# Packing a mixture of experts: places counted in strips of 32, ranks of 96 beside ranks of 32

## The chip, the core and the metric

The kernel runs on one core of a Trainium2 chip. The engines that matter here are TensorE (PE, with its weight loads shown apart as PEld), VectorE (DVE), ScalarE (ACT), GpSimd (POOL) and SyncE (SP), whose queue issues the loads of weights. The metric is the device time of one execution in microseconds, the median of several runs.

## What is computed

Two layers follow each other on 512 tokens of 1024 features, all in float32. The first has a gated delta-rule mixer and then a mixture of experts; the second a state-space and convolution mixer and an MLP. The change touches the mixture of experts alone. In the reference it is:

```python
scores = sigmoid(hf @ router_w)                 # 64 experts
...                                             # groups, then the best 6 experts of a token
top_w = top_w / sum(top_w) * 2.5
def expert_block(args):
    tok, e = args
    return swiglu(h_pad[tok], w_gate[e], w_up[e], w_down[e])
...
routed = zeros((t + 1, d)).at[slot_tok].add(out * slot_w)[:t]
return routed + swiglu(hf, s_gate, s_up, s_down)   # the shared expert
```

An expert has gate and up matrices of 1024 x 256 and a down matrix of 256 x 1024, 3 MB together; 64 of them are 192 MB, and all are loaded once.

## The kernel before

**The plan.** How many tokens an expert gets is known only at run time. The kernel sorts the experts by that count, so rank 0 is the fullest, and gives each rank a fixed number of places (`CAPS`); tokens beyond them go to the loop `beyond`, which runs no turn on these inputs. Four experts (60 to 63) are `fix`ed: they have a block of 128 places of their own and come first, before the sorting is done. The other 60 ranks are laid into blocks of up to 128 rows by `plan()`: ranks 0 to 17 alone (`NPAIR`; ranks 0, 1 and 2 take two blocks each), ranks 18 to 43 in pairs, two strips of 64 rows to a block (`NQUAD`), and ranks 44 to 59 in fours, strips of 32. That makes 42 blocks: 4 fixed, 21 of one rank, 13 pairs, 4 fours. The list `BLOCKS` alternates blocks of one rank, fullest first, with blocks of several, emptiest first, so most of the stage is one-rank, pair, one-rank, pair; its last blocks are the pair of ranks 18 and 19 and then rank 17 alone.

**A block.** `blocks` (line 1638 and on) walks the list. For a block, `load_block` issues the loads of its experts' weights on SyncE's queue (line 1519; three loads of 1 MB an expert: two halves of gate and up, then down; first part 0 of every expert of the block, then part 1, then part 2). `gather` brings the tokens' rows (POOL, line 1587, two blocks ahead). `ffn` does the arithmetic: `pt_x` transposes the rows (line 142) and `modulate` writes `xT`; `gu` (line 139) has 8 steps over the features, in each of them one matmul for each strip of the block, 512 columns wide, gate and up side by side; ACT and DVE make `h`; `pt_h` transposes it; `py` has two halves of 512 columns, each with 2 steps and again one matmul a strip. A matmul of a strip of 32 or 64 rows has its place in the array by `tile_position=(0, a)`, where a is the strip's first row; a block of one rank has none. `scatter` (POOL, line 1633) adds each strip's rows to `yacc` in DRAM.

In the profile `gub<-ewrank,xTb 128*64` is such a matmul of `gu` with 64 rows, `pyb` one of `py`; `ewx` is a slot of the ring that was first another tensor. A float32 matmul has two records.

**What sets the order.** The code is written block by block; a scheduler then orders each engine's queue. In many pairs it issues `py` of the first strips, then the rest of the next block's `pt_x`, then the remaining `py`. The weights live in a ring of slots of 1 MB: 10, two more once the tables of places are made, three more from `SECOND` on (block 17 of the list, when two leave), and ten again in the last `LEAVE` = 6 blocks. A load waits until its slot's last reader is done and until the eighth load before it has landed.

The shared expert (`su`, `sg`, `spy`) is spread over the blocks by `hooks`. After the last block, `sums` are read back from `yacc`, added and normed, and PE goes on with `ptn` of the second layer.

The three lines of `ffn` around which the change turns are:

```python
m = n // len(ws)
parts = [(i * m, (i + 1) * m) for i in range(len(ws))]
...
    for (a, b), w in zip(parts, ws):
```

Of the kernel before, what the change touches and what calls it, by code (L numbers as in the profile page):

```python
# [16 lines left out]
P = 128  # L17
# [809 lines left out]
def block_one(k, pool, early, two, route):  # L827
# [7 lines left out]
    with ExitStack() as es:  # L835
# [217 lines left out]
NE = 64  # L1053
NFIX = 4
NRK = NE - NFIX
NPAIR, NQUAD = 18, 44
CAPS = [256, 192, 152, 128, 124, 118, 108, 100, 92, 88, 86, 82, 79, 76, 75, 72, 70, 68, 64, 64, 62, 62, 59, 57, 56, 54, 54, 52, 51,
        50, 49, 46, 45, 44, 44, 43, 42, 41, 41, 40, 39, 38, 37, 37, 32, 32, 32, 31, 30, 30, 28, 26, 25, 23, 22, 20, 20, 18, 17, 16]
CAPS = [-(-c // 16) * 16 for c in CAPS]
NOV = 72  # L1060
LEAVE = 6
LAST = 0
AHEAD = 2
RING = 10
RINGX = 3
# [4 lines left out]

def plan():

    fixed = [(e, P, [("fix", NRK + e)]) for e in range(NFIX)]
    one, more, b, r = [], [], NFIX, 0
    while r < NRK:
        n = 1 if r < NPAIR else 2 if r < NQUAD else 4
        c = CAPS[r]
        if n == 1:
            g = []
            while c > 0:  # L1080
                g.append((b, min(c, P), [("rank", r)]))
                c -= P
                b += 1
            one.append(g)
        else:
            more.append([(b, P, [("rank", r + i) for i in range(n)])])
            assert max(CAPS[r:r + n]) <= P // n
            b += 1
        r += n

    more = more[::-1]
    m = len(one) - LAST
    order, i, j = [], 0, 0
    while i < m or j < len(more):
        if i >= m or j < len(more) and j * m <= i * len(more):
            order.append(more[j])
# [12 lines left out]
CST2 = ["iota", "low", "col", "base", "cap"]


def const2():
    j = np.arange(P)[:, None]
    i = np.arange(P)[None, :]
    t = {
        "iota": np.broadcast_to(i, (P, P)),
        "low": (j < i),
        "col": np.broadcast_to(j, (P, P)),

        "base": np.broadcast_to(np.resize(np.concatenate([NFIX * P + np.cumsum([0] + STEP[:NRK - 1]), np.arange(NFIX) * P]), P)[:, None], (P, P)),  # L1120
        "cap": np.broadcast_to(np.resize(np.array(CAPS + [P] * NFIX), P)[:, None], (P, P)),
    }
    return np.concatenate([np.asarray(t[n], np.float32) for n in CST2], 1)
# [22 lines left out]
class Moe:  # L1146
# [423 lines left out]

    def parts(self, n):

        b, rows, whos = BLOCKS[n]
        if n < NFIX:
            return [(0, self.tokf[0:rows, b:b + 1])]
        if len(whos) == 1:
            return [(0, self.tok[0:rows, b:b + 1])]
        m = P // len(whos)
        t = {0: self.tok, 32: self.tok2, 64: self.tok3, 96: self.tok4}
        return [(a, t[a][0:CAPS[r], b:b + 1]) for a, (_, r) in zip(range(0, P, m), whos)]  # L1580

    def gather(self, idx):

# [5 lines left out]
                                            bounds_check=511, oob_is_err=False)  # L1589
        return X  # L1590

    def ffn(self, pool, ps, ws, X, wslot, n, nm):

        k, nc = self.k, self.k.nc
        xT = pool.tile([P, 8, P], F32, tag="xT", name="xT" + nm)
        for q in range(2):
            pt = ps.tile([P, 4, P], F32, tag="tp", name=f"pt_x{nm}{q}")
            for i in range(4):
                nc.tensor.transpose(pt[:, i, 0:n], X[0:n, (4 * q + i) * P:(4 * q + i + 1) * P], k.ident[0:n, 0:n])
            self.modulate(pt[:, :, 0:n], q, lambda c: xT[:, c, 0:n])  # L1600
        m = n // len(ws)
        parts = [(i * m, (i + 1) * m) for i in range(len(ws))]
        gu = ps.tile([P, 512], F32, tag="gu", name="gu" + nm)
        for i in range(8):
# [12 lines left out]
        y = pool.tile([P, 1024], F32, tag="y", name="y" + nm, bufs=3)  # L1617
        for half in range(2):
            cs = slice(512 * half, 512 * half + 512)
            py = ps.tile([P, 512], F32, tag="py", name=f"py{nm}{half}")  # L1620
            for c in range(2):
                for (a, b), w in zip(parts, ws):
                    nc.tensor.matmul(py[a:b, :], hT[:, c, a:b], w[2][:, c * 1024 + half * 512:c * 1024 + half * 512 + 512],
                                     start=(c == 0), stop=(c == 1), **({"tile_position": (0, a)} if len(ws) > 1 else {}))
            nc.vector.tensor_tensor(y[0:n, cs], py[0:n], self.gt2[0:n, cs], ALU.mult)  # L1625
        return y

# [9 lines left out]
    def blocks(self, bp, ps, hooks, span):  # L1637

        pend, Xs = self.pend, self.Xs
        for n in range(*span):  # L1640
            b, rows, whos = BLOCKS[n]
            if n == len(BLOCKS) - LEAVE:
                for f in self.first:
                    self.slots.remove(f)
            if n == len(BLOCKS) - LAST:

                last = [self.load(w[0]) for _, _, w in BLOCKS[n:]]
                for i in ((0, 1), (2,)):
                    for w in last:
                        for j in i:  # L1650
                            w[1](j)
            ws = self.load_block(whos)
# [12 lines left out]

    def beyond(self, bp, ps):
        k, nc, tc = self.k, self.k.nc, self.k.tc
        V = nc.vector
        n = nc.values_load(self.nov, min_val=0, max_val=NOV)
        with tc.For_i(0, n, 1) as i:  # L1670
            sl = bp.tile([P, 1], I32, tag="sl", name="sl_o")
            sw = bp.tile([P, 1], F32, tag="sw", name="sw_o")
            V.tensor_copy(sl, self.tok[:, bass.ds(i + NB, 1)])
            V.tensor_copy(sw, self.tw[:, bass.ds(i + NB, 1)])
            v = nc.sync.value_load(self.eov[:, bass.ds(i, 1)], min_val=0, max_val=NE - 1)
            src = k.I["ew"][bass.ds(v, 1)].rearrange("a p f -> p (a f)")
            ws = []
            for q in range(3):
# [739 lines left out]
def body(nc, tc, I, out, dbg=None):  # L2418
    k = Ctx()
    k.nc, k.tc, k.I, k.out = Nc(tc), tc, I, out  # L2420
    pool = lambda es, nm, bufs, **kw: es.enter_context(tc.tile_pool(name=nm, bufs=bufs, reuse_waits="tile", **kw))
    with ExitStack() as es:
# [11 lines left out]
        with ExitStack() as e1:  # L2434
# [7 lines left out]
            for _, _, whos in BLOCKS[:3]:  # L2442
                moe.load_block(whos)
# [32 lines left out]
```

## Time and profile before

| | us |
|---|---|
| median of three runs | 2032.55 |
| the runs | 2032.37, 2033.91, 2032.55 |
| the profiled execution | 2032.14 |
| its span in the trace | 2030.3 |
| PE busy | 1827.9 (90%) |
| ACT busy | 596.5 (29%) |
| DVE busy | 995.1 (49%) |
| POOL busy | 503.4 (25%) |

All durations below come from the one profiled execution, so sums are made against its 2032.14 us; 1.8 us of it lie outside the span. The page divides the span into 40 slices of 50.8 us and gives for each slice the busy share of every engine in tenths. A row of a timeline gives the start, the time from the first start to the last end of the instructions put together in it, the engine, the line, and what was written from what; its bracket says how long the engine was idle before and which engine it waited for. The mean granted clock of PE is 0.958 over the span.

### The profile page before, as it was taken

How to read it: one execution, taken by the hardware profiler on the slowest of the kernel's cores; microseconds unless marked ns; L12 is line 12 of the kernel's file. 1: busy time of each engine (PE TensorE's matmuls, PEld its weight loads, DVE VectorE, ACT ScalarE, POOL GpSimd, SP SyncE). 2: the span in 40 equal slices, each digit the busy share in tenths (PEclk: the TensorE clock that was granted, in tenths of full speed). 3: DMA queues.
4: the chain of work that ended last, by engine and by line, in shares of the span. 5: the costliest groups of instructions: out<-in, count | busy, mean ns of one | idle time of the engine just before them, and what ended most of it. 6: DMA issues, size and time to landing. Idle time of an engine off the chain costs nothing. (4 is left out here: it accounts for less than half of the span.)

```text
span 2030.3 us, 24186 instructions
## 1 busy us (share of the span) xinstructions
PE 1827.9 (90%) x8465; PEld 1235.3 (61%) x8465; DVE 995.1 (49%) x2205; ACT 596.5 (29%) x1124; POOL 503.4 (25%) x408
## 2 busy tenths in 40 slices
PE   5997778987889999989999984999999999999998
PEld 3785556876644333333333333888888788888886
DVE  4789955667866222352222226667433453323352
ACT  5443311213323111111111114343323334323441
POOL 1314343542322221212121215333100113101300
PEclk9998888997979999999999996999999999999999
DMA  8354353226478999999999973333332432333241
GB/s 309 122 184 148 89 161 97 81 71 215 157 295 297 354 370 351 346 392 389 365 369 370 374 267 114 122 94 92 108 99 84 134 100 94 93 94 104 78 140 42
DMA packets 135569, 394.01 MB, mean 194 GB/s; under 512 B 46932, under 2 KB 59348, under 8 KB 109080
## 3 DMA queue, kind: packets, MB, share of 16 engines
q1 hardware_dynamic: 109608, 363.60, 50.6%
q0 software_dynamic: 12016, 27.29, 5.5%
q10 hardware_dynamic: 13824, 1.58, 0.5%
q8 instruction: 67, 1.10, 0.2%
q14 instruction: 54, 0.44, 0.1%
HBM read 365.13 MB, written 39.06 MB: 199 GB/s over the span
## 5 line engine op out<-in xcount | busy, mean ns | idle before, releaser
L139 PE MATMUL gub<-ewrank,xTb 128*64 128x512 f32 (+5 forms) x960 | 266.4, 595 | 0.8 <-DMA ewrank<-ew 0.2
L274 DVE TENSOR_TENSOR wlo<-wraw,whi 128x1024 fp32r<-128x1024 f32 (+1 forms) x103 | 120.9, 1174 | 138.4 <-ACT whi L273 137.5
L139 PEld LDWEIGHTS gub<-ewrank,xTb 128*64 128x64 f32 (+5 forms) x960 | 89.0, 140 | 159.5 <-issue 146.7
L273 ACT CAST whi<-wraw 128x1024 fp32r<-128x1024 f32 (+1 forms) x115 | 113.9, 991 | 211.9 <-PE psi L139 50.6
L139 PE MATMUL pyb<-ewrank,hTb 128*64 128x512 f32 (+5 forms) x440 | 154.6, 609 | 3.3 <-DMA ewrank<-ew 1.3
L139 PE MATMUL psi<-xnh,whi 128*128 128x512 f32 (+1 forms) x368 | 142.6, 388 | 0.0
L139 PE MATMUL psi<-xnl,whi 128*128 128x512 f32 (+1 forms) x368 | 141.1, 384 | 0.0
L1633 POOL DMA_INDIRECT yacc<-yb,tok x63 | 89.0, 1412 | 171.3 <-DVE yb L1625 121.5
L1611 DVE SCALAR_TENSOR_TENSOR hb<-gub,tw,sgb 128x256 f32<-128x256 f32 (+5 forms) x38 | 18.3, 482 | 230.8 <-ACT sgb L1609 230.8
L1335 ACT ACTIVATE xTb<-pt_xb,B,A 128x128 f32<-128x128 f32 (+5 forms) x168 | 74.1, 445 | 170.3 <-DVE xTb L1337 169.0
L139 PE MATMUL psi<-xnh,wlo 128*128 128x512 f32 (+1 forms) x296 | 113.2, 383 | 0.0
L1587 POOL DMA_INDIRECT X<-hrow,tok x38 | 39.5, 1041 | 292.0 <-PE pt_xb L142 286.4
L1337 DVE TENSOR_SCALAR xTb<-pt_xb,A,B 128x128 f32<-128x128 f32 (+5 forms) x168 | 65.6, 393 | 89.3 <-PE pt_xb L142 52.9
L2399 POOL TENSOR_TENSOR fr<-fr 128x512 f32<-128x512 f32 x32 | 48.6, 1519 | 238.2 <-ACT fr L2398 238.2
L139 PE MATMUL psf<-xml,whi 128*128 128x512 f32 (+1 forms) x272 | 102.5, 377 | 0.2 <-DVE xml L274 0.2
L139 PE MATMUL psf<-xmh,whi 128*128 128x512 f32 (+1 forms) x272 | 102.4, 377 | 0.2 <-ACT xmh L273 0.2
L139 PE MATMUL psf<-xmh,wlo 128*128 128x512 f32 (+1 forms) x272 | 102.4, 377 | 0.0
L1609 ACT ACTIVATE sgb<-gub 128x256 f32<-128x256 f32 (+5 forms) x42 | 16.0, 382 | 262.4 <-PE gub L139 262.4
L139 PEld LDWEIGHTS pyb<-ewrank,hTb 128*64 128x64 f32 (+5 forms) x440 | 46.7, 143 | 76.0 <-issue 64.7
L1625 DVE TENSOR_TENSOR yb<-pyb,gt 128x512 f32<-128x512 f32 (+5 forms) x84 | 58.0, 690 | 70.2 <-PE pyb L139 70.0
L139 PEld LDWEIGHTS psi<-xnh,whi 128*128 128x128 f32 x368 | 69.9, 191 | 13.8 <-ACT xnh L2264 0.4
L139 PEld LDWEIGHTS psi<-xnl,whi 128*128 128x128 f32 x368 | 70.0, 190 | 13.2
(752 smaller groups left out, 4026.0 us busy)
## 6 DMA issues: line engine op xcount, KB each, us to landing
ewrank<-ew SPq DMA_DIRECT2D x168, 1024.0 KB, 25.1
wraw<-w_in SPq DMA_DIRECT2D x59, 512.0 KB, 3.6
wraw<-ff SPq DMA_DIRECT2D x32, 512.0 KB, 3.5
wf<-ff SPq DMA_DIRECT2D x64, 256.0 KB, 2.7
wm<-w_mod SPq DMA_DIRECT2D x28, 512.0 KB, 7.8
ewfix<-ew SPq DMA_DIRECT2D x12, 1024.0 KB, 15.4
ewx<-ew SPq DMA_DIRECT2D x12, 1024.0 KB, 20.2
wm<-w_mod SPq DMA_DIRECT2D x10, 1024.0 KB, 6.2
```

Of the source, the lines that this page charges most:

```text
L139: return self._done(self.eng.matmul(out, lhsT, rhs, **kw), rate, rhs)
L273: nc.scalar.copy(hi, raw)
L274: (eng or nc.vector).tensor_tensor(lo, raw, hi.bitcast(F32), ALU.subtract)
L1335: nc.scalar.activation(dst(c), pt[:, i, :], AF.Identity, scale=sa, bias=sb)
L1337: nc.vector.tensor_scalar(dst(c), pt[:, i, :], sa, sb, ALU.mult, ALU.add)
L1587: self.k.nc.gpsimd.indirect_dma_start(out=X[0:idx.shape[0]], out_offset=None, in_=self.hrow, in_offset=bass.IndirectOffsetOnAxis(ap=idx, a ...
L1609: nc.scalar.activation(sg[0:n], gu[0:n, 0:256], AF.Silu)
L1611: nc.vector.scalar_tensor_tensor(h[0:n], gu[0:n, 256:512], wslot[0:n], sg[0:n], ALU.mult, ALU.mult)
L1625: nc.vector.tensor_tensor(y[0:n, cs], py[0:n], self.gt2[0:n, cs], ALU.mult)
L1633: self.k.nc.gpsimd.indirect_dma_start(out=self.yacc[self.nsc % 2], out_offset=bass.IndirectOffsetOnAxis(ap=idx, axis=0), in_=y[a:a + n], i ...
L2399: nc.gpsimd.tensor_tensor(r, r, r, ALU.mult)
```

## The change

Places are counted in strips of 32: `STRIPS` gives each rank 8, 6, 5, five times 4, ten times 3, 26 times 2 and 16 times 1, and `CAPS` is 32 times that, nowhere less than before. `plan()` lays ranks into blocks without holes: rank 0 has two blocks; ranks 1 and 2 with one rank of 32 share three (128 of rank 1; 64 of rank 1 and 64 of rank 2; 96 of rank 2 and 32 of rank 44); ranks 3 to 7 have one each; ranks 8 to 17, of 96 places, share their block with one rank of 32 each; 26 ranks of 64 make 13 pairs; the five ranks of 32 that are left make one block of four and one block of rank 59 alone. That is 39 blocks: 4 fixed, 9 of one rank, 14 of two strips of 64, 1 of four, 11 of 96 and 32. A block's entry now holds the first row and the length of each part. In `ffn` a part of 96 rows becomes two strips, 64 and 32.

The list still alternates groups of `few` and `many`, but the groups are longer: after rank 59 alone and rank 0 come the four, two pairs, the three blocks of ranks 1, 2 and 44, four pairs, rank 3, three pairs, rank 4, four pairs, rank 5, and then the blocks of 96 and 32 with ranks 6 and 7 among them; the last is that of ranks 8 and 45.

```diff
-NPAIR, NQUAD = 18, 44
-CAPS = [256, 192, 152, 128, 124, 118, 108, 100, 92, 88, 86, 82, 79, 76, 75, 72, 70, 68, 64, 64, 62, 62, 59, 57, 56, 54, 54, 52, 51,
...
-CAPS = [-(-c // 16) * 16 for c in CAPS]
-NOV = 72
+
+STRIPS = [8, 6, 5] + [4] * 5 + [3] * 10 + [2] * 26 + [1] * 16
+CAPS = [32 * s for s in STRIPS]
+NOV = 73
...
+        for r in ranks:
+            base[r], n = P * b[0] + at, CAPS[r]
+            todo.remove(r)
+            while n > 0:
+                if at % P == 0:
+                    g.append((b[0] + at // P, []))
+                m = min(n, P - at % P)
+                g[-1][1].append((at % P, m, ("rank", r)))
+                at, n = at + m, n - m
...
+    few += [group([0]), group([1, 2] + ones(1))] + [group([r]) for r in range(3, n4)]
+    for n in (3, 2, 1):
+        while any(STRIPS[r] == n for r in todo):
+            g = [r for r in todo if STRIPS[r] == n][:{3: 1, 2: 2, 1: 4}[n]]
+            many.append(group(g + (ones(1) if n == 3 else [])))
...
-        m = n // len(ws)
-        parts = [(i * m, (i + 1) * m) for i in range(len(ws))]
+
+        strips = [(a + i, min(a + m, a + i + s), w) for (a, m, _), w in zip(parts, ws)
+                  for i, s in ([(0, 64), (64, 32)] if m == 96 else [(0, m)])]
...
-            for (a, b), w in zip(parts, ws):
+            for a, b, w in strips:
                 nc.tensor.matmul(gu[a:b, :], xT[:, i, a:b], w[i // 4][:, (i % 4) * 512:(i % 4) * 512 + 512],
-                                 start=(i == 0), stop=(i == 7), **({"tile_position": (0, a)} if len(ws) > 1 else {}))
+                                 start=(i == 0), stop=(i == 7), **({"tile_position": (0, a)} if len(strips) > 1 else {}))
```

The same is done in `py`. `parts`, `base` and the loop over blocks follow the new form of an entry; the branch for `LAST`, which was 0, goes.

Rank 8 shows what this does on PE. Before, in its own block 15, with 96 rows and no place in the array (`gub15`, `pt_hb15`, `pyb15`; the last number of a name is the program's own, and x4 are four in a row):

```order
L139 MATMUL gub15_7310<-ewrank8_0_7282,xTb15_7291 96x512 x4
L139 MATMUL gub15_7310<-ewrank8_1_7284,xTb15_7291 96x512 x4
L142 MATMUL pt_hb15_7323<-cst_60,hb15_7321 128x96 x2
L139 MATMUL pyb150_7329<-ewrank8_2_7286,hTb15_7326 96x512 x2
L139 MATMUL pyb151_7333<-ewrank8_2_7286,hTb15_7326 96x512 x2
```

After, in block 14 with rank 45, the first steps of `gub14`:

```order
L139 MATMUL gub14_8806<-ewrank8_0_8775,xTb14_8787 64x512
L139 MATMUL gub14_8806<-ewrank8_0_8775,xTb14_8787 32x512
L139 MATMUL gub14_8806<-ewrank45_0_8777,xTb14_8787 32x512
L139 MATMUL gub14_8806<-ewrank8_0_8775,xTb14_8787 64x512
L139 MATMUL gub14_8806<-ewrank8_0_8775,xTb14_8787 32x512
L139 MATMUL gub14_8806<-ewrank45_0_8777,xTb14_8787 32x512
```

Each step has now a matmul of 64 rows and one of 32 rows with rank 8's weights and one of 32 rows with rank 45's.

The second place is `py` of a block of two ranks that the scheduler divides. Before, the pair of ranks 18 and 19, on PE near the end of the stage:

```order
L139 MATMUL pyb250_8760<-ewrank18_2_8707,hTb25_8757 64x512
L139 MATMUL pyb251_8766<-ewrank18_2_8707,hTb25_8757 64x512
L142 MATMUL pt_xb241_8801<-cst_60,X2_4567 128x80 x2
L139 MATMUL pyb250_8760<-ewrank19_2_8709,hTb25_8757 64x512
L139 MATMUL pyb250_8760<-ewrank18_2_8707,hTb25_8757 64x512
L139 MATMUL pyb250_8760<-ewrank19_2_8709,hTb25_8757 64x512
L139 MATMUL pyb251_8766<-ewrank19_2_8709,hTb25_8757 64x512
L139 MATMUL pyb251_8766<-ewrank18_2_8707,hTb25_8757 64x512
L139 MATMUL pyb251_8766<-ewrank19_2_8709,hTb25_8757 64x512
```

After, PE's last block of the stage, ranks 8 and 45:

```order
L139 MATMUL pyb140_8841<-ewrank8_2_8783,hTb14_8838 64x512
L139 MATMUL pyb140_8841<-ewrank8_2_8783,hTb14_8838 32x512
L139 MATMUL pyb141_8849<-ewrank8_2_8783,hTb14_8838 64x512
L139 MATMUL pyb141_8849<-ewrank8_2_8783,hTb14_8838 32x512
L139 MATMUL pyb140_8841<-ewrank45_2_8785,hTb14_8838 32x512
L139 MATMUL pyb140_8841<-ewrank8_2_8783,hTb14_8838 64x512
L139 MATMUL pyb140_8841<-ewrank8_2_8783,hTb14_8838 32x512
L139 MATMUL pyb140_8841<-ewrank45_2_8785,hTb14_8838 32x512
L139 MATMUL pyb141_8849<-ewrank45_2_8785,hTb14_8838 32x512
L139 MATMUL pyb141_8849<-ewrank8_2_8783,hTb14_8838 64x512
L139 MATMUL pyb141_8849<-ewrank8_2_8783,hTb14_8838 32x512
L139 MATMUL pyb141_8849<-ewrank45_2_8785,hTb14_8838 32x512
```

Where strips of 64 alternated with strips of 64, the widths now go 64, 32, 64, 32 in the first four and change again in the other eight.

The third place is SyncE's queue where rank 0 comes. Before, from the loads of the four to rank 1's first parts:

```order
L1519 DMA ewx1_4984<-ew 128x2048
L1519 DMA ewrank57_2_5154<-ew 128x2048
L1519 DMA ewrank58_2_5156<-ew 128x2048
L1519 DMA ewrank59_2_5158<-ew 128x2048
L1519 DMA ewrank0_0_5258<-ew 128x2048
L1519 DMA ewrank0_1_5260<-ew 128x2048
L1519 DMA ewrank0_2_5262<-ew 128x2048
L1519 DMA ewrank1_0_5387<-ew 128x2048
```

After, from rank 59 alone to the middle of the four's first parts:

```order
L1522 DMA ewrank59_0_5108<-ew 128x2048
L1522 DMA ewrank59_1_5110<-ew 128x2048
L1522 DMA ewrank59_2_5112<-ew 128x2048
L1522 DMA ewrank0_0_5176<-ew 128x2048
L1522 DMA ewrank0_1_5178<-ew 128x2048
L1522 DMA ewrank0_2_5180<-ew 128x2048
L1522 DMA ewrank55_0_5326<-ew 128x2048
L1522 DMA ewx1_4984<-ew 128x2048
L1522 DMA ewx1_4984<-ew 128x2048
L1522 DMA ewrank58_0_5330<-ew 128x2048
L1522 DMA ewrank55_1_5332<-ew 128x2048
```

The four's loads stood ahead of rank 0's; now rank 0's stand ahead of them, and rank 59's ahead of those.

## Rows read from the trace of the kernel before

**Rows 1.** The page's second part: busy tenths of PE and DMA in 40 slices.

```profile
PE   5997778987889999989999984999999999999998
...
DMA  8354353226478999999999973333332432333241
```

**Rows 2.** The windows of the expert stage: busy us, granted clock, DMA share, GB/s.

```profile
680.00:720.00 40.00, 36.95 (x154) 14.26 (x153) 9.91 (x21) 7.22 (x18) 7.70 (x6) 1.00 0.94 321
...
760.00:800.00 40.00, 37.62 (x173) 15.47 (x173) 8.40 (x17) 6.53 (x15) 8.22 (x7) 1.00 0.86 340
...
840.00:880.00 40.00, 34.72 (x134) 13.81 (x132) 23.00 (x108) 6.47 (x15) 7.71 (x7) 1.00 0.90 326
880.00:1200.00 320.00, 291.05 (x1030) 106.84 (x1031) 83.68 (x188) 56.36 (x136) 67.64 (x53) 0.99 1.01 372
```

**Rows 3.** SyncE's timeline, 590 to 1190: start, us from first to last, count.

```profile
855.57 326.96 SPq L1519 DMA_DIRECT2D ewrank<-ew  x108
...
1100.45 82.09 SPq L1519 DMA_DIRECT2D ewrank<-ew  x27
```

**Rows 4.** The page's sixth part: loads of experts, KB each, us to landing.

```profile
ewrank<-ew SPq DMA_DIRECT2D x168, 1024.0 KB, 25.1
```

**Rows 5.** PE's timeline at the end of the expert stage: start, us, names.

```profile
1187.98 7.09 PE L139 MATMUL gub<-ewrank,xTb 128*64 128x512 f32 x32
...
1197.09 1.93 PE L139 MATMUL pyb<-ewrank,hTb 128*64 128x512 f32 x4
...
1199.23 3.65 PE L139 MATMUL pyb<-ewrank,hTb 128*64 128x512 f32 x12
1202.81 7.09 PE L139 MATMUL gub<-ewrank,xTb 128*80 128x512 f32 x16
...
1211.68 3.66 PE L139 MATMUL pyb<-ewrank,hTb 128*80 128x512 f32 x8 [0.44 <-ACT hTb L1616]
1248.20 2.39 PE L142 MATMUL ptn<-cst,sums 128*128 128x128 f32 x10 [32.85 <-ACT sums L2255]
```

**Rows 6.** The groups of instructions from 880 to 1200, weight loads of gub.

```profile
L139 PEld LDWEIGHTS gub<-ewrank,xTb 128*64 128x64 f32 (+3 forms) x528 | 52.4, 144 | 98.6 <-issue 90.5 <-DMA ewrank<-ew 4.5 <-ACT xTb L1335 3.4
```

**Rows 7.** PE's timeline earlier in the stage: one expert, four, a pair.

```profile
661.65 7.11 PE L139 MATMUL gub<-ewrank,xTb 128*128 128x512 f32 x16 [0.22 <-DMA ewrank<-ew]
...
674.68 1.88 PE L139 MATMUL gub<-ewrank,xTb 128*128 128x512 f32 x4
...
766.17 7.07 PE L139 MATMUL gub<-ewrank,xTb 128*32 128x512 f32 x64
...
840.09 7.09 PE L139 MATMUL gub<-ewrank,xTb 128*64 128x512 f32 x32
...
852.83 3.70 PE L139 MATMUL spy<-ewshared,shh 128*128 128x512 f32 x8
...
856.81 1.45 PE L139 MATMUL gub<-ewrank,xTb 128*128 128x512 f32 x3
```

**Rows 8.** PE's timeline where widths change, weight load (PEld) of pw last.

```profile
816.21 1.90 PE L139 MATMUL pyb<-ewrank,hTb 128*32 128x512 f32 x4
818.04 1.98 PE L139 MATMUL spy<-ewshared,shh 128*128 128x512 f32 x4
819.96 0.62 PE L139 MATMUL pyb<-ewrank,hTb 128*32 128x512 f32 x1
...
1295.79 1.92 PE L139 MATMUL pf<-smQ,smbst 128*16 128x128 f32 x16
...
1296.23 1.47 PE L139 MATMUL pf<-smQ,smbst 128*16 128x128 f32 x12
1297.64 1.20 PE L139 MATMUL pw<-ssU,smwin 128*64 128x64 f32 x32
...
1297.64 0.26 PEld L139 LDWEIGHTS pw<-ssU,smwin 128*64 128x64 f32 x6 [0.21 <-issue]
```

**Rows 9.** POOL's timeline at the end of the stage, the last scatter.

```profile
1216.35 1.42 POOL L1633 DMA_INDIRECT yacc<-yb,tok  x1 [9.33 <-DVEq L1670]
```

More of the change, by code (lines that the diff above doesn't have):

```diff
@@ L1055 @@
 NRK = NE - NFIX
-NPAIR, NQUAD = 18, 44
-CAPS = [256, 192, 152, 128, 124, 118, 108, 100, 92, 88, 86, 82, 79, 76, 75, 72, 70, 68, 64, 64, 62, 62, 59, 57, 56, 54, 54, 52, 51,
-        50, 49, 46, 45, 44, 44, 43, 42, 41, 41, 40, 39, 38, 37, 37, 32, 32, 32, 31, 30, 30, 28, 26, 25, 23, 22, 20, 20, 18, 17, 16]
-CAPS = [-(-c // 16) * 16 for c in CAPS]
-NOV = 72
+STRIPS = [8, 6, 5] + [4] * 5 + [3] * 10 + [2] * 26 + [1] * 16
+CAPS = [32 * s for s in STRIPS]
+NOV = 73
 LEAVE = 6
-LAST = 0
 AHEAD = 2
@@ L1071, in plan @@
 def plan():
[L1073 to L1096, printed above, removed]
+    few, many, base, todo = [], [], {}, list(range(NRK))
+    b = [NFIX]
+    def group(ranks):
+        g, at = [], 0
+        for r in ranks:
[7 more added lines that the diff above has]
+                at, n = at + m, n - m
+        b[0] += len(g)
+        return [(i, max(a + n for a, n, _ in ps), ps) for i, ps in g]
@@ new lines, in plan @@
+    n4 = sum(s > 3 for s in STRIPS)
+    ones = lambda n: [r for r in todo if STRIPS[r] == 1][:n]
+    few += [group([0]), group([1, 2] + ones(1))] + [group([r]) for r in range(3, n4)]
[3 more added lines that the diff above has]
+            many.append(group(g + (ones(1) if n == 3 else [])))
+    many = many[::-1]
+    order, i, j = [(e, P, [(0, P, ("fix", NRK + e))]) for e in range(NFIX)], 0, 0
@@ L1097, in plan @@
+    while i < len(few) or j < len(many):
+        if i >= len(few) or j < len(many) and j * len(few) <= i * len(many):
+            order += many[j]
             j += 1
         else:
-            order.append(one[i])
+            order += few[i]
             i += 1
-    order += one[m:]
-    return fixed + [x for g in order for x in g], b
-BLOCKS, NB = plan()
+    return order, b[0], [base[r] for r in range(NRK)]
+BLOCKS, NB, BASE = plan()
 NBT = NB + NOV
 NSLOT = NB * P
-STEP = [-(-c // P) * P if r < NPAIR else 64 if r < NQUAD else 32 for r, c in enumerate(CAPS)] + [P] * NFIX
@@ L1118, in const2 @@
         "col": np.broadcast_to(j, (P, P)),
-        "base": np.broadcast_to(np.resize(np.concatenate([NFIX * P + np.cumsum([0] + STEP[:NRK - 1]), np.arange(NFIX) * P]), P)[:, None], (P, P)),
+        "base": np.broadcast_to(np.resize(np.array(BASE + [P * e for e in range(NFIX)]), P)[:, None], (P, P)),
         "cap": np.broadcast_to(np.resize(np.array(CAPS + [P] * NFIX), P)[:, None], (P, P)),
@@ L1571, in parts @@
     def parts(self, n):
-        b, rows, whos = BLOCKS[n]
+        b, rows, ps = BLOCKS[n]
         if n < NFIX:
             return [(0, self.tokf[0:rows, b:b + 1])]
-        if len(whos) == 1:
-            return [(0, self.tok[0:rows, b:b + 1])]
-        m = P // len(whos)
         t = {0: self.tok, 32: self.tok2, 64: self.tok3, 96: self.tok4}
-        return [(a, t[a][0:CAPS[r], b:b + 1]) for a, (_, r) in zip(range(0, P, m), whos)]
+        return [(a, t[a][0:m, b:b + 1]) for a, m, _ in ps]
     def gather(self, idx):
@@ L1590, in gather, with ffn @@
         return X
-    def ffn(self, pool, ps, ws, X, wslot, n, nm):
+    def ffn(self, pool, ps, ws, X, wslot, n, parts, nm):
         k, nc = self.k, self.k.nc
@@ L1621, in ffn @@
             for c in range(2):
-                for (a, b), w in zip(parts, ws):
+                for a, b, w in strips:
                     nc.tensor.matmul(py[a:b, :], hT[:, c, a:b], w[2][:, c * 1024 + half * 512:c * 1024 + half * 512 + 512],
-                                     start=(c == 0), stop=(c == 1), **({"tile_position": (0, a)} if len(ws) > 1 else {}))
+                                     start=(c == 0), stop=(c == 1), **({"tile_position": (0, a)} if len(strips) > 1 else {}))
             nc.vector.tensor_tensor(y[0:n, cs], py[0:n], self.gt2[0:n, cs], ALU.mult)
@@ L1640, in blocks @@
         for n in range(*span):
-            b, rows, whos = BLOCKS[n]
+            b, rows, parts = BLOCKS[n]
             if n == len(BLOCKS) - LEAVE:
@@ L1644, in blocks @@
                     self.slots.remove(f)
[L1645 to L1652, printed above, removed]
+            ws = self.load_block([w for _, _, w in parts])
             self.rows_ahead(min(n + AHEAD, NFIX if span[0] == 0 else len(BLOCKS)))
-            y = self.ffn(bp, ps, ws, Xs[n], (self.twf if n < NFIX else self.tw)[:, b:b + 1], rows, f"b{b}")
+            y = self.ffn(bp, ps, ws, Xs[n], (self.twf if n < NFIX else self.tw)[:, b:b + 1], rows, parts, f"b{b}")
             part = self.parts(n)
@@ L1682, in beyond @@
             X = self.gather(sl)
-            y = self.ffn(bp, ps, [ws], X, sw, P, "o")
+            y = self.ffn(bp, ps, [ws], X, sw, P, [(0, P, None)], "o")
             self.scatter(y, [(0, sl)])
@@ L2441, in body @@
             ps = Psum(pool(e1, "psM", 1, space=PSUM), tp=3, gu=2, py=3)
-            for _, _, whos in BLOCKS[:3]:
-                moe.load_block(whos)
+            for _, _, parts in BLOCKS[:3]:
+                moe.load_block([w for _, _, w in parts])
             moe.places(ps, bp.tile([P, 1024], F32, tag="y", name="keys", bufs=3))
```

## The prediction

> **What bounds the kernel now.** I read the slices of the whole span first, 50.8 us each [rows 1]: TensorE (PE) stands at eights and nines from the 13th slice (609 us) on, but for the 25th (1218 to 1269), and the DMA tenths are nines from the 14th to the 23rd, some 510 us. That stretch is the expert stage, the only one the change touches. The windows of it [rows 2] say that it is close to a tie: from 880 to 1200 PE is busy 291 of 320 us and the DMA share is 1.01; in three earlier windows the share falls to 0.94, 0.86 and 0.90, so transfers also lose time. Then SyncE's queue: the last 27 loads of 1 MB are issued in 82.09 us, 82.09/26 = 3.16 us from one to the next, and 108 in 326.96 us, 3.06 [rows 3]; I take 3.14 for a load near the end. The last issue is at 1182.5, a load lands 25.1 us after its issue, so near 1207, and PE ends the last block at 1215.3 [rows 3 to 5]. On the other side the weight loads of `gub` wait only 4.5 us for transfers in those 320 us [rows 6]. So PE's own work decides, with transfers a few us behind it; whichever of the two grows sets the end. What follows (scatter, sums, `ptn` 32.85 us after PE's last) hangs on the last `pyb` [rows 5].
>
> **The change, part by part.** All is set against the profiled execution, 2032.14 us (span 2030.3), 0.4 us under the median 2032.55.
>
> *Blocks removed.* A block costs PE much the same whatever its strips, since strips of one width run side by side: `gub` takes 7.11 us for one expert, 7.07 for four strips (64 records), 7.09 for two (32) [rows 5, 7]. From one `gub` to the next: 13.03 for one expert (661.65 to 674.68); 14.83 for a pair whose `pyb` is issued in two pieces, 1.93 + 3.65 (1187.98 to 1202.81); 13.1 for a pair issued in one (840.09 to 856.81 is 16.72, less 3.6 of the shared expert's `spy` in it) [rows 5, 7]. A block of four goes as 13.1: same `gub`, same kind of `pyb`.
> Before: 21 x 13.0 + 4 x 13.1 + 2 x 13.1 + 11 x 14.83 = 514.7 us. After, were 96+32 like a pair: 9 x 13.0 + 1 x 13.1 + 7 x 13.1 + 7 x 14.83 (14 blocks of two strips of 64) + 10 x 14.83 + 1 x 13.1 = 487.0. That is **-27.7 us** of PE. Which are issued in one piece I counted in the order of the instructions.
>
> *The 96+32 blocks.* Eleven of them issue strips of 64, 32 and 32 in turn, 24 matmuls in `gub`, two records each. No block before mixes widths on disjoint columns, so the price must be bounded. Lower end: the strips overlap as equal ones do, and this costs nothing (below nothing is excluded, since no strip takes fewer records than the 0.43 us steps already counted). Upper end: PE waits for each width to finish. Three rows speak to it. Between 32-wide `pyb` and 128-wide `spy`, 816.21 to 818.04 is 1.83 and 818.04 to 819.96 is 1.92 us [rows 8]; four records there span 1.90 with 0.6 of the last, so a step is 0.43, eight are 3.43 and each change of width costs (3.75 - 3.43)/2 = 0.16. From 16-wide `pf` to 64-wide `pw`, four `pf` records take 0.44 (1295.79 to 1296.23), 0.11 each; twelve more should end at 1297.55 and `pw` starts at 1297.64, 0.09 later; its weight load starts only at 1297.64 too, put down to "issue", where other weight loads run ahead [rows 8]. So a change of width holds even the weight load until the array is empty. These rows have shared columns, so they show the wait and not that disjoint columns wait also. But a wait that keeps back the weight load looks like one of the whole array, and I take the upper end as likeliest, with 0.13 per change (mean of 0.09 and 0.16).
> The Trainium skill ("TensorEngine Tiling (Array Packing)", Tiling Modes, Key Properties) says that changing the tiling mode, not just the tile, drains TensorE. It speaks against this change; the rows on the changes of width agree as far as they go, and by it the sum is the upper end, without it the lower.
> Price: in `gub`, each of 8 steps has the 64 alone and then the two 32s together: 8 x (4 records x 0.429 + 2 x 0.13) = 15.8 against 7.09, +8.7. In `pyb` the first piece (64, 32, 64, 32) has four turns of 0.858 (two records) and four changes, 3.95 against 1.93, +2.0; the second has six turns and five changes, 5.8 against 3.65, +2.15. So +12.9 a block, 27.7 instead of 14.83, and **+142 us** for eleven. With 25 changes a block, 0.09 instead of 0.13 gives -11, 0.16 gives +8.
>
> *Transfers.* The same 192 MB of experts are loaded, in another order. A 96+32 block needs two experts, 6 x 3.14 = 18.8 us, under its 27.7: there the ring stays full and PE waits for nothing. In the first 23 blocks of ranks, up to the run of mixed ones, 111 loads x 3.14 = 349 us stand against PE's 328 of expert blocks (the sum above up to there) and some 58 of the shared expert's (four of 16 matmuls like a `gub`, eight like `spy`, 3.7 [rows 7]); level on the whole, but pairs now come four in a row (75 us of loads against 52 to 59 of PE). PE waits between nothing (10 to 13 slots loaded ahead cover a run) and 23 us (one run, nothing ahead); I take **+8**, nearer to the 4.5 of now [rows 6].
>
> *Tail and small edits.* The last block scatters two parts instead of one; POOL's last one takes 1.42 us [rows 9]: **+1.4**. SyncE reads experts' numbers ahead of loads as before. Gathers fall from 42 to 39 and scatter parts stay 67, on a POOL idle most of the stage; the tables are 2 columns smaller; new capacities are no smaller, so the overflow loop still runs no turn. Nothing for these: PE's block time hides them, and they only shrink.
>
> *Sum:* -27.7 + 142 + 8 + 1.4 = +123.7, and 2032.14 + 123.7 is about **2156 us**.
>
> **Rivals.**
> *A: the strips overlap, or a change costs its 0.13 alone.* Then a 96+32 block takes PE 14.8 to 18.1 (25 x 0.13), under the 18.8 of its loads, and transfers set the end: the 27.7 us buy nothing, as the same megabytes follow one another. What they lose decides. Rank 0's three slots are held through two blocks, 26 us, while only nine of the next four-block's twelve loads fit in the ring beside it: I reckon 15 us of idle queue near 666 to 680, some of it already lost now in the 0.86 and 0.90 windows [rows 2], and 4 to 8 more where two single experts no longer alternate with pairs. By slots and 3.14 a load the last landing comes some 16 us later; PE then needs 5 us after it instead of 8 to 9, since only the last `pyb` is left: +12, and +1.4. That is **2045**, slower too, but by 0.6%. For it: equal strips do overlap [rows 5, 7]. Against: the weight load that did not run ahead [rows 8].
> The Trainium skill ("TensorE: Matmul & The Clock Gate", Part 3) has column tiles run concurrently, with 3 tiles of 32 some 2.4 times faster. This trace agrees for equal widths, where the 16 + 16 records of a pair fit in 7.09 us; for 64 beside 32 no run here shows it. Were it so, rival A's time follows.
> *B: overlap, and the queue loses nothing: faster.* The place is the ring's refill at rank 0 and in the two low windows: 760 to 800 loses 0.14 x 40 = 5.6 us, 840 to 880 4.0, 680 to 720 2.4 [rows 2], together 12.0. If fewer one-expert blocks let the ring run at 1.01 throughout, the last landing comes 12 earlier and PE follows in 5 us instead of 8 to 9, -15.5, with the +1.4 to **2018**. It decides where a 96+32 block stays under 18.8 us and rank 0's hold costs under some 10 us.
>
> **How the numbers follow.** The forecast, drain: 0.70, with 2138 to 2179 as its own range (-11 and -8 for cheap changes and no waits, +8 and +15 the other way). A: 0.20. B: 0.05. Something between A and B, within 4 us (0.2%, about what a measurement of this kernel can tell from no change): 0.05. So faster 0.05, same 0.05, slower 0.90. For 8 in 10 the forecast's range alone is short, so it reaches down past A with some 7 us for its transfer terms, to 2038; what is left out is B, the middle and the edges.
>
> **What would show it.** In the changed kernel, `gub` of a 96+32 block near 15.8 us and block to block near 27.7; the 64 strip's record starting only after the 32s of the step before. If those `gub` take 7.1, A or B holds: then look at DMA's share from 640 to 760 and at the last landing against PE's end. One-expert blocks and pairs must stay at 13.0 and 13.1 to 14.8, and the tail from the last `pyb` to `ptn` at 32.9 + 1.4. Wrong would be the forecast also if PE's clock fell in the mixed blocks, or if loads, now ahead, still made PE wait.

## The result

The changed kernel takes 2172.34 us (2169.29 to 2174.51), the kernel before 2032.46 beside it: a ratio of 1.0695, 95% interval 1.068 to 1.0709. The forecast was 2156 in a range of 2038 to 2179, slower. Its profiled execution has a span of 2171.6 us, 141.3 more than before.

The slices of the changed kernel, 54.3 us each, against [rows 1] (first PE's busy tenths, then DMA's):

```profile
PE   6988599878799899888999998399999999999998
...
DMA  7454362254677959899976662343232342333241
```

PE stays at eights and nines to the end of the expert stage (the 25th slice). DMA is at 7 and 6 from the 21st to the 24th and at 2 in the 25th, where before it stood at nines for ten slices on end. The end of the stage is now PE's. The window of the mixed blocks says the same (busy us, granted clock, DMA share, GB/s):

```profile
1040.00:1340.00 300.00, 287.32 (x861) 64.03 (x859) 40.11 (x82) 29.94 (x70) 39.12 (x30) 1.00 0.68 237
```

PE is busy 287 of 300 us, its clock stays at 1.00, and the DMA share is 0.68.

PE's timeline over two blocks of 96 and 32, the last but one and the last (start, us from the first start to the last end, names, idle before):

```profile
1297.09 15.95 PE L139 MATMUL gub<-ewrank,xTb 128*64 128x512 f32 x48
1314.13 0.44 PE L142 MATMUL pt_hb<-cst,hb 128*128 128x128 f32 x2 [1.09 <-DVE hb L1612]
...
1315.08 4.03 PE L139 MATMUL pyb<-ewrank,hTb 128*64 128x512 f32 x8
1319.04 0.33 PE L142 MATMUL pt_xb<-cst,X 128*128 128x128 f32 x1
1319.30 5.87 PE L139 MATMUL pyb<-ewrank,hTb 128*32 128x512 f32 x16
1325.10 0.55 PE L142 MATMUL pt_xb<-cst,X 128*128 128x128 f32 x3
1325.58 15.95 PE L139 MATMUL gub<-ewrank,xTb 128*64 128x512 f32 x48
...
1343.54 8.86 PE L139 MATMUL pyb<-ewrank,hTb 128*64 128x512 f32 x24 [0.52 <-ACT hTb L1617]
1390.41 2.39 PE L142 MATMUL ptn<-cst,sums 128*128 128x128 f32 x10 [38.00 <-ACT sums L2249]
```

Against [rows 5]: `gub` takes 15.95 us where a pair's took 7.09 and one expert's 7.09; `pyb`'s pieces take 3.96 and 5.80 to the next row where they took 1.86 and 3.58; block to block is 28.49 us against 14.83. PE is idle 38.00 us before `ptn`, not 32.85.

Two steps of that `gub`, seen by its weight loads (PEld):

```profile
1326.58 0.14 PEld L139 LDWEIGHTS gub<-ewrank,xTb 128*32 128x32 f32 x4 [0.81 <-issue]
1327.56 0.19 PEld L139 LDWEIGHTS gub<-ewrank,xTb 128*64 128x64 f32 x2 [0.84 <-ACT xTb L1338]
1328.56 0.14 PEld L139 LDWEIGHTS gub<-ewrank,xTb 128*32 128x32 f32 x4 [0.81 <-issue]
```

The four weights of the two strips of 32 go in together, then nothing for 0.84 us, then both of the 64, then nothing for 0.81. One width's weights come only when the other's matmuls are through: from 32 to 64 to 32 is 0.98 and 1.00 us, so a step takes 1.98 where strips of one width need 0.86. (The second row names ACT's writing of `xTb`, but the slice of it that this step reads was written at 1316; in the later steps the same 0.84 is put down to "issue".)

The waits for weights, PEld's and PE's own on `gub`, summed over the changed kernel (us, times, longest):

```profile
PEld gub L139 <- DMA ewrank<-ew: 20.7, 10, 3.2
...
PE gub L139 <- DMA ewrank<-ew: 13.0, 10, 2.3
```

PEld's came to 4.5 us in the main stretch before [rows 6], 4.6 over that whole run. None of those here lies in the run of mixed blocks from 1043 us on.

### The profile page after: what moved, and what is told of

It is laid out like the page before. It is cut to its first block, busy times and chain, and to the rows that moved or that the text cites. A ratio compares the mean times of both kernels' runs of the same rounds, so it can differ in the third digit from the quotient of the medians.

```text
span 2171.6 us, 24583 instructions
## 1 busy us (share of the span) xinstructions
PE 1955.9 (90%) x8699; PEld 1231.7 (57%) x8699; DVE 988.2 (46%) x2184; ACT 591.3 (27%) x1106; POOL 509.2 (23%) x405
## 4 chain that ended last, share of the span: by engine, by line
PE 65%; DVE 12%; DMA 9%; issue 3%; ACT 2%; POOL 1%; SPq 0%; another core or an unknown queue 0%; ACTq 0%; DVEq 0%; POOLq 0%
PE gub L139 13%; PE psi L139 11%; PE pof L139 8%; PE psf L139 8%; PE pyb L139 8%; DMA ewrank<-ew 6%; PE psco L139 2%; DVE cfa L746 2%; PE poo L139 1%; PE pxca L139 1%; PE psga L139 1%; PE psgb L139 1%; PE psp L139 1%; PE psy L139 1%; PE po L139 1%
## 5 line engine op out<-in xcount | busy, mean ns | idle before, releaser
L139 PE MATMUL gub<-ewrank,xTb 128*64 128x512 f32 (+2 forms) x1136 | 354.8, 614 | 13.4 <-DMA ewrank<-ew 13.0
L139 PEld LDWEIGHTS gub<-ewrank,xTb 128*64 128x64 f32 (+2 forms) x1136 | 88.7, 133 | 249.8 <-issue 212.9
L139 PE MATMUL pyb<-ewrank,hTb 128*64 128x512 f32 (+2 forms) x544 | 196.7, 605 | 3.1 <-ACT hTb L1617 0.9
L1612 DVE SCALAR_TENSOR_TENSOR hb<-gub,tw,sgb 128x256 f32<-128x256 f32 (+1 forms) x35 | 16.9, 483 | 318.8 <-ACT sgb L1610 318.8
L1338 ACT ACTIVATE xTb<-pt_xb,B,A 128x128 f32<-128x128 f32 (+1 forms) x156 | 70.5, 455 | 269.6 <-DVE xTb L1340 268.6
L1626 DVE TENSOR_TENSOR yb<-pyb,gt 128x512 f32<-128x512 f32 (+1 forms) x78 | 53.9, 691 | 146.9 <-PE pyb L139 146.7
L139 PEld LDWEIGHTS pyb<-ewrank,hTb 128*64 128x64 f32 (+2 forms) x544 | 46.8, 130 | 118.4 <-issue 106.8
L1610 ACT ACTIVATE sgb<-gub 128x256 f32<-128x256 f32 (+1 forms) x39 | 15.0, 383 | 313.6 <-PE gub L139 313.6
L1340 DVE TENSOR_SCALAR xTb<-pt_xb,A,B 128x128 f32<-128x128 f32 (+1 forms) x156 | 62.9, 405 | 76.2 <-PE pt_xb L142 40.8
L139 PEld LDWEIGHTS psi<-xnl,whi 128*128 128x128 f32 x368 | 69.6, 189 | 13.2
```

The lines of the kernel that those rows point to most:

```text
L139: return self._done(self.eng.matmul(out, lhsT, rhs, **kw), rate, rhs)
L1338: nc.scalar.activation(dst(c), pt[:, i, :], AF.Identity, scale=sa, bias=sb)
L1340: nc.vector.tensor_scalar(dst(c), pt[:, i, :], sa, sb, ALU.mult, ALU.add)
```

## Experiments

The runs are called e1 to e10. Two theories stand against each other at first: that the mixing of widths makes the loss, and that the new plan, with its order of loads, does.

### One width in the changed kernel (e1)

```diff
-                  for i, s in ([(0, 64), (64, 32)] if m == 96 else [(0, m)])]
+                  for i, s in ([(0, 32), (32, 32), (64, 32)] if m == 96 else [(0, m)])]
```

> The changed kernel with one edit: a part of 96 rows is cut into three strips of 32 instead of 64 and 32, so that a block of 96 and 32 is four strips of one width (32 matmuls in gu instead of 24). Theory (PE empties itself between widths, and 64 does not run beside 32): gub of these blocks falls from 15.9 to 7.1 us, block to block from 28.5 to 14.8 to 15.0, and the stage is bound by the loads again: 2040 to 2050 us. Rival (the order of loads and the longer runs of pairs make most of the loss): gub falls, but PE waits for weights instead and the time stays above 2100. Rival (the number of matmuls costs, not their widths): gub rises above 15.9 and the time above 2172.

Measured: 2052.22 us, ratio to before 1.0103 (1.0083 to 1.0123). That is 120 us less than the changed kernel, with more matmuls, so the widths make nearly all of its loss. It is 2 us above the range written down. What is left, 21 us, is transfers and some 4 us of tail (below). The windows of this run (busy us, granted clock, DMA share, GB/s), against [rows 2]:

```profile
640.00:680.00 40.00, 35.01 (x98) 13.75 (x97) 18.93 (x101) 6.71 (x19) 6.07 (x5) 0.96 0.68 246
...
760.00:800.00 40.00, 37.64 (x196) 14.18 (x195) 7.62 (x15) 5.77 (x13) 7.74 (x6) 1.00 0.77 255
...
840.00:880.00 40.00, 36.16 (x141) 14.47 (x138) 18.35 (x75) 6.39 (x15) 7.81 (x6) 1.00 0.82 298
880.00:1200.00 320.00, 274.76 (x1407) 94.06 (x1405) 80.30 (x202) 49.68 (x116) 66.43 (x52) 0.98 1.01 380
```

From 880 to 1200 PE is busy 275 us instead of 291 and the share is still 1.01: PE's gain is there, and it buys nothing. In the three windows ahead of it the shares are lower than before: 0.86 and 0.90 stand in [rows 2], and the kernel before from 640 to 680 has

```profile
640.00:680.00 40.00, 35.87 (x171) 15.35 (x172) 15.56 (x66) 7.87 (x19) 11.60 (x9) 0.96 0.99 365
```

The blocks of 96 and 32 did not come down to the 14.8 to 15.0 us expected. The `gub` of the first of them (782.26), which waits for nothing, takes 7.07; the later ones wait for weights and go in 15.6 to 19.7 us, about what the loads of two experts take (18.8 at 3.14 a load). PE's waits on `gub` in this run, where the changed kernel had 13.0:

```profile
PE gub L139 <- DMA ewrank<-ew: 26.5, 17, 2.3
```

So PE does wait for weights instead, as the first rival has it, but the time does not stay above 2100.

### Widths in groups (e2)

```diff
-        for i in range(8):
-            for a, b, w in strips:
+        widths = sorted({b - a for a, b, _ in strips}, reverse=True)
+        for i, (a, b, w) in [(i, s) for v in widths for i in range(8) for s in strips if s[1] - s[0] == v]:
```

and the same over `py`'s two steps.

> The changed kernel with the matmuls of gu and py put in order by width: all eight steps of the strip of 64 first, then all eight of the two strips of 32 (py: both steps of 64, then of 32). Two costs come apart: strips that can't run side by side, and changes of width. Theory: gu still has 16 turns of 0.858 us, but one change instead of 15, so 13.8 to 13.9 us against 15.9; with py some 4 to 4.6 us less a block, 44 to 50 us in eleven, 2122 to 2130 us. Rival (the change of width is what costs, and without changes strips overlap again as equal ones do): gub near 7 to 8 us and 2045 to 2060. Rival (the changes cost nothing, the turns are all): within 4 us of 2172.

Measured: 2132.39 us, 40 less than the changed kernel; the range was missed by 2. PE's timeline of one block in this run:

```profile
1236.38 14.07 PE L139 MATMUL gub<-ewrank,xTb 128*64 128x512 f32 x48
1251.55 0.44 PE L142 MATMUL pt_hb<-cst,hb 128*128 128x128 f32 x2 [1.09 <-DVE hb L1612]
...
1252.79 8.32 PE L139 MATMUL pyb<-ewrank,hTb 128*64 128x512 f32 x24
1261.03 14.07 PE L139 MATMUL gub<-ewrank,xTb 128*64 128x512 f32 x48
```

`gub` goes from 15.95 to 14.07 with 14 changes fewer: 1.88/14 = 0.134 us for a change, where 0.13 was taken. The other 6.98 us of its excess over 7.09 are turns that no longer lie beside each other. Block to block is 24.65, 3.84 us less; what `gub` does not give, 1.96, comes from `pyb` and the transposes between its pieces. The expected 4 to 4.6 was a little high: `pyb` still changes three times, since each half has its own 64 and 32.

### The mixing alone, in the kernel before (e3)

```diff
+        strips = [(a, b, w) for (a, b), w in zip(parts, ws)]
+        if len(ws) == 2:
+            strips = [(a, a + s, ws[a // 64]) for a, s in [(0, 64), (64, 32), (96, 32)]]
...
```

and the loops of `gu` and `py` go over `strips`.

> The kernel before, its plan and its 42 blocks untouched, but the second strip of every pair is issued as two strips of 32 (64, 32, 32 in gu and py). Width mixing alone, without the new plan. Theory: 13 pairs lengthen by 13 to 13.7 us each, less the some 10 us that the pairs now wait for weights: 2180 to 2205 us. Rival (the new plan and order make the loss): within 10 us of 2032.

Measured: 2162.15 us, ratio 1.0663 (1.0636 to 1.0691). The new plan is not needed for the loss. But the size was missed, by 18 us at least. A pair of this run:

```profile
1269.16 15.95 PE L139 MATMUL gub<-ewrank,xTb 128*64 128x512 f32 x48
...
1287.13 1.93 PE L139 MATMUL pyb<-ewrank,hTb 128*64 128x512 f32 x4
1288.99 0.36 PE L142 MATMUL pt_xb<-cst,X 80*128 80x80 f32 x2
1289.28 5.88 PE L139 MATMUL pyb<-ewrank,hTb 128*32 128x512 f32 x20
1295.09 1.09 PE L139 MATMUL gub<-ewrank,xTb 128*80 128x512 f32 x2
```

`gub` is the same 15.95, yet the first piece of `pyb` holds only the first expert's 64 and stays at 1.93, as before [rows 5]. So a pair goes from 14.83 to 25.93, +11.1 and not 13 to 13.7. Thirteen of them are 144, and the time rose by 131. Most of the difference was already in the pairs: five of them took 15.58 to 16.51 us before, with waits for weights, some 6 us in all above the others' 14.88, and another had a wait for DVE that is 5 us shorter here (below).

### The control: narrow strips alone (e4)

```diff
+            strips = [(a, a + s, ws[a // 64]) for a, s in [(0, 32), (32, 32), (64, 32), (96, 32)]]
```

in the place of e3's list, all else as in e3.

> Control for the run before: the kernel before with every pair issued as four strips of 32, two for each expert, so one width and twice the matmuls. Theory: gub stays 7.1 us, and the time within 4 us of 2032. Rival (more and narrower matmuls cost in themselves): gub above 8 us and over 2045.

Measured: 2031.16 us against 2030.99, ratio 0.9999 (0.9988 to 1.001). Twice the matmuls, half as wide, cost nothing.

### The mixing in gu alone (e10)

```diff
-            for a, b, w in strips:
+            for a, b, w in ([(q, q + s, strips[q // 32][2]) for q, s in ((0, 64), (64, 32), (96, 32))] if any(p[1] == 96 for p in parts) else strips):
                 nc.tensor.matmul(gu[a:b, :], ...
```

in the kernel of e1, with four strips of 32.

> The changed kernel's order and blocks, widths mixed (64, 32, 32) in gu alone; py of the blocks of 96 and 32 in four strips of 32. It parts the price of the mixing by place. Theory (every turn that can't lie beside another costs, gu 8.9 us a block, py 4.3, and half a microsecond where transposes stand between widths): block to block 23.6 to 23.9 us instead of 28.5, time 2115 to 2126. Rival (a block's price is paid once, for the change as such): below 2080 or above 2150.

Measured: 2121.51 us, in the range. A block of it on PE:

```profile
1231.39 15.95 PE L139 MATMUL gub<-ewrank,xTb 128*64 128x512 f32 x48
...
1249.39 1.92 PE L139 MATMUL pyb<-ewrank,hTb 128*32 128x512 f32 x12
...
1251.49 3.62 PE L139 MATMUL pyb<-ewrank,hTb 128*32 128x512 f32 x20
1255.04 0.55 PE L142 MATMUL pt_xb<-cst,X 128*128 128x128 f32 x3
1255.52 7.03 PE L139 MATMUL gub<-ewrank,xTb 128*64 128x512 f32 x20
```

Block to block is 24.13, 0.23 above what was written. `pyb`'s pieces are back to 1.92 and 3.62, so mixing in `py` costs 28.49 - 24.13 = 4.36 us a block. A pair of the changed kernel that waits for nothing takes 15.31 (below), so mixing in `gu` costs 8.82. The two add up: eleven times 4.36 is 48, and the times differ by 51.

### Where the rest lies: the four ahead of rank 0 (e5)

All the runs from here to e8 have four strips of 32 and change only the list, by a line after it: `order = order[:NFIX] + [order[i] for i in (...)]`. An index is a block's place in the changed kernel's list: 4 is rank 59, 5 and 6 are rank 0, 7 is the four. Here the indices are 7, 5, 6, 4 and then 8 to 38.

> The run with four strips of 32 (e1), and one edit: the list starts with the block of four, then rank 0's two blocks, then rank 59 alone, instead of rank 59, rank 0, the four. In e1 the DMA share is 0.68 from 640 to 680, where the kernel before has 0.99: 12 us of transfers lost. Theory (rank 0's three slots, held for two blocks, keep the four's twelve loads out of the ring): the share there goes back above 0.9, and as transfers bound the rest, the time falls by 6 to 12 us, to 2040 to 2046. Rival (lost time early is made up later, as PE bounds): within 4 us of 2052.

Measured: 2041.98 us, ratio 1.0045 (1.0029 to 1.0061), 10 less than e1. The window says why:

```profile
640.00:680.00 40.00, 35.57 (x171) 14.74 (x170) 17.14 (x84) 8.07 (x20) 9.96 (x8) 0.96 0.99 373
```

The share is 0.99 again instead of 0.68, 12.4 us of transfers, and 10.2 us of them come out at the end.

### The whole list spread (e6)

The indices are 7, 5, 6, 4, 8, 9, 13 to 16, 18, 19, 20, 10, 11, 12, 22, 23, 17, 24, 25, 21, 27, 28, 29, 26, 31, 32, 33, 30, 34, 36, 35, 37, 38.

> e1 with the whole list in an order that keeps the ring from filling: the four, rank 0, rank 59, then six pairs under the shared expert's work, three more, the three blocks of ranks 1, 2 and 44, and one-rank blocks after every second or third block of two experts. Same blocks, same matmuls. Theory (e1 is bound by transfers, and the 19 us by which it is slower than before are transfers lost from 640 to 680, 760 to 800 and 840 to 880): shares near 1.0 in these windows and 2020 to 2032 us, at or below the kernel before. Rival (each load takes as long as the queue lets it, the share of 1.0 is no room): above 2045.

Measured: 2026.31 us, ratio 0.9966 (0.9951 to 0.9982): faster than the kernel before by 0.3%, and the fastest of this study together with e7; its ten runs and those of before overlap. Its windows:

```profile
640.00:680.00 40.00, 34.86 (x169) 14.35 (x168) 18.12 (x92) 8.08 (x20) 9.97 (x8) 0.96 0.97 369
...
760.00:800.00 40.00, 37.66 (x148) 15.10 (x147) 7.58 (x15) 5.36 (x13) 7.81 (x6) 1.00 1.00 394
...
840.00:880.00 40.00, 37.76 (x132) 14.89 (x131) 18.56 (x72) 6.09 (x14) 10.52 (x8) 1.00 0.74 255
```

Two of three shares came up as expected; that of 840 to 880 did not, it is 0.74. So some 10 us of transfers are still lost there; no run tried to win them.

### The last block (e7 and e8)

First in the spread list, where rank 7's block (index 35) goes to the end:

> e6 with rank 7's block of one expert moved to the end, so that the last scatter has one part instead of two. Theory (the second part costs the wait of 2.5 us for the first one's issue and its own landing): the idle time of PE before ptn falls from 37.2 to 38.0 us to 32.9 to 33.5, but the last expert's part of the work after the last landing grows by about as much as it saves, so within 4 us of e6. Rival (the tail decides alone): 4 to 6 us under e6.

Measured: 2026.09 us, e6 again. Then alone, in the list of the changed kernel:

> e1 with that one move alone: rank 7's block to the end, all else in the changed kernel's order. Theory: PE idle before ptn 32.9 to 33.5 instead of 37.2, time 2044 to 2052. Rival (the longer tail is not the second part's but the stage's): idle stays at 37 us.

Measured: 2049.09 us, 3 less than e1. PE's first `ptn` in e6, e7 and e8, in that order:

```profile
1244.90 2.40 PE L142 MATMUL ptn<-cst,sums 128*128 128x128 f32 x10 [38.59 <-ACT sums L2250]
```

```profile
1242.57 2.40 PE L142 MATMUL ptn<-cst,sums 128*128 128x128 f32 x10 [33.44 <-ACT sums L2250]
```

```profile
1269.46 2.39 PE L142 MATMUL ptn<-cst,sums 128*128 128x128 f32 x10 [34.14 <-ACT sums L2250]
```

With one part in the last scatter the idle time falls by 5.2 us in e7. In e8 it falls by 3.1 against e1's 37.2, 0.6 short of what was written. So most of the longer tail is the second part's: e1's is 4.4 us above the 32.85 of before, e8's still 1.3. The time follows less: in e7 PE ends its last block 2.8 us later than in e6 (1209.13 against 1206.31), so `ptn` starts 2.3 earlier; the profiled executions differ by 2.1 (2026.04 against 2028.16), and the medians of ten not at all. The 3 us between e8 and e1 lie within the spread of e1's four runs, 2045.89 to 2053.93.

### The spread list under mixed widths (e9)

> The changed kernel with its mixed widths (64, 32, 32) left in, and the order of e6 for the list. The forecast put 8 us on waits for weights; in the changed kernel the block-to-block times of the two-strip blocks ahead of the mixed run show some 33 us above 13.1 to 14.8. Theory (these waits come from four pairs in a row with the ring behind, and PE sets the rest): they fall to 8 to 12 us as in e6, and the time by 20 to 30 us, to 2142 to 2152. Rival (PE is the bound, the order is worth nothing): 2168 to 2176.

Measured: 2144.75 us, 27.6 less than the changed kernel, in the range. In its trace no matmul waits for an expert's weights. With PE as the bound of the mixed blocks, the order of the loads is still worth 28 us, since the waits lie ahead of them.

## Why the forecast was right, and what it mis-sized

**Strips of two widths don't run side by side, and each change costs: shown.** The step of 1.98 us in the weight loads, e3 (mixing alone loses 131 us in the kernel before), e4 (narrow strips alone lose nothing) and e1 (one width gives 120 of the 140 us back) leave no room for another main cause. The price in `gub` was put at 15.8 us and is 15.95 to the last end; `pyb`'s at 3.95 and 5.8, and they are 3.96 and 5.80; a change at 0.13, and e2 gives 0.134. Taking the upper end because the weight load of `pw` was held back [rows 8] was the choice that carried the forecast. That rule of the Trainium skill ("TensorEngine Tiling (Array Packing)", Tiling Modes, Key Properties: a change of mode drains TensorE) agrees with this trace and holds here on disjoint columns too. Whether strips of 64 and 32 could stand in the array at once if nothing drained is open: no run can part the two.

**The blocks removed: overstated.** -27.7 us took a block in two pieces at a pair's 14.83 [rows 5]. In the changed kernel such a pair, waiting for nothing, takes 15.31. PE's timeline of pairs in the changed kernel, the first and the third with waits:

```profile
923.19 1.04 PE L139 MATMUL gub<-ewrank,xTb 128*64 128x512 f32 x2 [0.73 <-DMA ewrank<-ew]
925.38 5.35 PE L139 MATMUL gub<-ewrank,xTb 128*64 128x512 f32 x16 [1.15 <-DMA ewrank<-ew]
932.18 3.65 PE L139 MATMUL gub<-ewrank,xTb 128*64 128x512 f32 x14 [1.45 <-DMA ewrank<-ew]
...
956.96 7.09 PE L139 MATMUL gub<-ewrank,xTb 128*64 128x512 f32 x32
...
968.33 3.65 PE L139 MATMUL pyb<-ewrank,hTb 128*64 128x512 f32 x12
971.90 0.44 PE L142 MATMUL pt_xb<-cst,X 128*128 128x128 f32 x2
972.27 1.07 PE L139 MATMUL gub<-ewrank,xTb 128*64 128x512 f32 x2
973.70 3.68 PE L139 MATMUL gub<-ewrank,xTb 128*64 128x512 f32 x16 [0.36 <-DMA ewrank<-ew]
```

The next block's last transposes now stand behind the second piece of `pyb`, where PE has no wait to put them under: 0.48 us a block, some 8 us in the sixteen blocks of this form (seven pairs and nine of 96 and 32). The scheduler put them there; the order of the changed kernel's instructions shows it, and the working did not count it.

**Eleven mixed blocks: right.** 28.49 - 15.31 = 13.2 us each against 12.9; 145 us with the last, against 142.

**Waits for weights: less than half of what they were.** I took 8, between 0 and 23; PEld's waits on `gub` rise from 4.6 us over the whole run to 20.7, by 16, and the blocks that wait lengthen by more, since the clock falls behind some waits (last section). The seven pairs in two pieces go from one `gub` to the next in 18.97, 20.37, 20.73, 15.31, 20.75, 16.03 and 21.15 us, 26 in all above 15.31 each; before, the pairs with waits had some 6 in all above 14.88. So +20. In e9 the pairs take 13.3 to 15.3, less the shared expert's work, and the time falls by 27.6. The step that failed is "nearer to the 4.5 of now": the two pairs behind the four and the later ones in the runs of three and four pairs wait for weights. Two counts behind that step were off. The shared expert has 80 records in these blocks, 34 us at 0.43, and not 58 (four of eight like `spy`, not eight); and the 38 experts ahead of the mixed run make 114 loads, 358 us, not 349. So PE's 328 + 34 stood level with the loads, where the working's own figures, 386 against 349, had 37 us in hand.

**Tail: a quarter of what it was.** +1.4 for one more issue on POOL; measured +5.15 (38.00 against 32.85). POOL's timeline of the changed kernel, then SyncE's:

```profile
1353.42 2.15 POOL L1634 DMA_INDIRECT yacc<-yb,tok  x1 [23.96 <-DVE yb L1626]
1355.87 1.32 POOL L1634 DMA_INDIRECT yacc<-yb,tok  x1 [0.30 <-DMA yacc<-yb,tok]
```

```profile
1364.50 11.30 SPq L2229 DMA_DIRECT2D sums<-yacc  x8
```

The first issue takes 2.15 us instead of 1.42 [rows 9], and the reading of `sums` starts 8.6 us after the second one's start; before, a start at 1216.35 was followed by `sums` at 1221.79, 5.4 us. I counted the issue and not its landing. Not all of this is the second part's: with one part of 128 rows the reading starts 6.8 (e7) and 7.0 us (e8) after the issue, and the 5.4 of before was one part of 80 rows; whether the rows make that difference no run shows.

**Two slow blocks of before: not counted.** The sum took every block of before at 13.0 to 14.83. Two were longer. One is a pair whose `pt_hb` waited for DVE, busy then with many small operations (23.00 us in 108 of them from 840 to 880 [rows 2]):

```profile
869.85 7.09 PE L139 MATMUL gub<-ewrank,xTb 128*64 128x512 f32 x32
883.42 0.69 PE L142 MATMUL pt_hb<-cst,hb 128*128 128x128 f32 x2 [6.48 <-DVE hb L1611]
```

It took 20.46 us where the sum has 13.1; in the changed kernel two blocks wait there, 1.45 and 2.23 us where 0.99 and 1.09 are usual. The other is the four at 802.82, 20.69 us with 3.5 of `spy` in it, 4 above 13.1; the one four that is left takes 13.35 there. Together some 10 us that the changed kernel saves.

Together: -27.7 + 8 + 145 + 20 + 5 - 10 = 140 against 141.3 of the span. The forecast is some 16 us low: the waits missed by 12, the blocks removed by 8, the tail by 4 and the mixed blocks by 3, and the 10 us that the working did not count hid a part of it. The mechanism and its price are not luck; that the small terms together missed by no more is luck in part.

**The rivals.** A's world is e1: one width makes it true. Its 2045 came out as 2052, and its places were right: the hold of rank 0 at 640 to 680 (e5 wins 10 us there) and the early windows. What it lacked is 3 us of the tail (4.4 where it had 1.4) and a few us of transfers. B's mechanism, a queue that loses less, exists as well: e6 reaches 2026.3 with it, though B's 2018 was too low: one window stays at 0.74, and the tail is 5.7 us longer instead of 1.4. Neither was open to the change as it stands, with its widths mixed.

## What to carry to other kernels

Pack strips of one width into TensorE's columns: in these float32 matmuls of 512 columns four of 32 cost what two of 64 do or one of 128 (7.07 to 7.11 us a `gub`), while a 64 beside two 32s costs more than twice as much (15.95). When PE's work is cut in a stage where transfers run level with it, ask first what the queue loses; here the same 39 blocks gave 2052 or 2026 us by the order of their loads alone. And a second scatter at the end of a chain is priced by when its rows have landed, not by its issue.

## What the runs showed beyond that

A wait for weights can cost more than its length. In the first pair above, 16 records of `gub` take 5.35 us after the second wait; in the third pair 16 take 3.68 (973.70). The window around the slow ones:

```profile
923.00:931.00 8.00, 6.39 (x18) 1.64 (x18) 0.41 (x1) 0.87 (x2) 3.63 (x3) 0.79 1.02 415
```

The granted clock has a mean of 0.79 there, so part of the stretch is at the lower of its two levels, 1.2 GHz, after PE had been idle 0.73 and 1.15 us with two records between. Gaps of about 1 us before each `pt_hb`, with a full `gub` and `pyb` on either side, leave it at 1.00 in three windows of [rows 2] and at 0.99 in the fourth.
